# Head and end of a macaron encoder layer: first weights in halves, gains with x's first tile, products of ones, other places for the rows of x, root from a partial sum

## Chip, core and metric

The kernel runs on one core of a Trainium2 chip. The metric is the device time of one execution in microseconds (us). Before the change the median of 3 runs is 2106.32 us (2105.33 to 2113.24).

## What is computed

One layer of an encoder, on 256 tokens of width 2048, all in float32. Cut to what matters here:

```python
def layer(x, mem, ...):                                  # x: (1, 256, 2048)
    h = rms_norm(x, ffn1_norm)
    x = x + 0.5 * swiglu_ffn(h, ffn1_w_in, ffn1_w_out)   # w_in: 2048 x 11264, w_out: 5632 x 2048
    ...                                                  # two token mixers, then cross-attention to mem
    h = rms_norm(x, ffn2_norm)
    x = x + 0.5 * swiglu_ffn(h, ffn2_w_in, ffn2_w_out)
    return rms_norm(x, final_norm)

def rms_norm(x, g):
    return x * lax.rsqrt(jnp.mean(x * x, axis=-1, keepdims=True) + 1e-6) * g

def swiglu_ffn(h, w_in, w_out):
    gate, up = jnp.split(h @ w_in, 2, axis=-1)
    return (jax.nn.silu(gate) * up) @ w_out
```

## The kernel before

Every float32 product is made of three products of a faster format: each operand is split into a high part (a copy in that format) and a low part (operand minus high part). So each weight tile of 128 x 1024 goes through one CAST on ACT (ScalarE, the high part) and one subtraction on DVE (VectorE, the low part) before PE (TensorE) uses it. `split` and `parts` do this; `gained` does the same for one 128 x 256 tile of the transposed x, times the gain of the norm.

The first feed-forward, class `FeedForward`, is where the program starts. `run` goes over the 16 tiles of 128 features of x (k = 0 to 15, called tile 0 to tile 15 below) for the first group of 512 gate and 512 up columns (group 0). For each tile the function `x_arrives` loads x's part (two tiles per DMA) and calls `gained`, `raw` loads the weight tile (512 KB), `parts` splits it, and `by_two` makes 12 products of 512 columns. Then follow ten more groups (`group`, from `seven` and `eight`), in which some pairs of tiles take fewer products by combined operands; `sides` prepares these from x in the first group, and `summed` prepares a tile whose low part a DMA of the POOL queue forms by adding in memory.

The factor of the norm, one number per token, is applied behind the products (`give`). So the sums of squares of x are only needed at the end of group 0: `x_squares` loads four pieces of x by rows (512 KB each) and squares them on ACT, and `x_root` makes the root.

Weight tiles land in nine buffers in turn: four of the pool `wraw` (named raw) and five parts of the tile `spare`. `x_squares` takes its buffers from `wraw` too. The split tiles have five buffers: three named hl and two of the tile ring. All these loads are issued by the SP queue (SyncE). The engines run in order, and a scheduler sets the order of each engine's instructions when the program is built, from its own estimate of times.

The end is the last quarter of the second feed-forward's output and the final norm. The first three quarters of each token's sum of squares (`sums`, one column per quarter) are known some 60 us before the end. `give` adds the four columns, takes a Sqrt on ACT, improves it by one step on DVE, and scales and stores the rows, for the two halves of the tokens (t = 0, then t = 1).

Of the kernel before, what the change touches and what calls it, by code (L numbers as in the profile page):

```python
# [40 lines left out]

PV_SIZES = [
    ("ffn1_norm", KD), ("mix_norm", KD), ("xattn_norm", KD), ("mem_norm", KD), ("ffn2_norm", KD),
# [23 lines left out]
def layer(ctx: ExitStack, tc: tile.TileContext, a: dict):  # L67
# [118 lines left out]
    nc.vector.memset(ones, 1.0)  # L186
    nc.scalar.activation(out=st.tile([P, 1], F32, name="warm"), in_=ones[:, 0:1], func=AF.Silu)
    ident = const.tile([P, P], F32, name="ident")
    make_identity(nc, ident)
    pv = const.tile([P, NPV], F32, name="pv")  # L190
    xt = ctx.enter_context(tc.tile_pool(name="xt", bufs=1))
    xT = xt.tile([P, KD, T], F32, name="xT", tag="x")
# [44 lines left out]
    def gained(dst, k, x, g):  # L237

        nc.scalar.activation(out=dst[:, k, 0], in_=x, func=AF.Copy, scale=g)
        nc.vector.scalar_tensor_tensor(  # L240
            out=dst[:, k, 1], in0=x, scalar=g, in1=dst[:, k, 0].bitcast(F32), op0=ALU.mult, op1=ALU.subtract
        )

# [55 lines left out]
    class FeedForward:  # L299
# [62 lines left out]
        def sides(self, i):  # L362
# [4 lines left out]
            for q in range(2):  # L367
                nc.scalar.activation(out=xg[:, q], in_=xT[:, k + q], func=AF.Copy, scale=col(self.gain, k + q))
# [86 lines left out]
        def run(self, before, after, root, more=None):  # L455
# [3 lines left out]
            for k in range(KD):  # L459
                before(k)  # L460
                w = self.parts(self.raw(0, k))
# [57 lines left out]
    head = PV["mix_norm"][0]  # L519

    def x_squares(c):

        raw = wraw.tile([P, 1024], F32, name="raw")
# [3 lines left out]
    with ExitStack() as stack:  # L527
        ff = FeedForward(stack, ("S1", "S0", "S2"), x_hl, "ffn1_norm", a["ffn1_w_in"], PATTERNS[0], SUMMED[0])

        def x_arrives(k):  # L530
            if k % 2 == 0:
                nc.sync.dma_start(out=xT[:, k:k + 2], in_=a["xT"][:, k:k + 2])
            if k == 0:
                nc.sync.dma_start(out=pv[:, :head], in_=a["pv"][:, :head])
            gained(x_hl, k, xT[:, k], col("ffn1_norm", k))

        def x_more(k):
            if k == 6:
                nc.sync.dma_start(out=pv[:, head:], in_=a["pv"][:, head:])
            if k in (5, 7, 9, 11):  # L540
                x_squares(k // 2 - 2)
# [14 lines left out]
        turns = ff.run(x_arrives, x_more, x_root, x_given)  # L556
# [423 lines left out]
    with ExitStack() as stack:  # L980
        ff = FeedForward(stack, ("S0", "S1", "S2"), x_hl, "ffn2_norm", a["ffn2_w_in"], PATTERNS[1], SUMMED[1])
# [29 lines left out]
        eps = st.tile([P, 1], F32, name="eps")  # L1011
        nc.vector.memset(eps, RMS_EPS)

# [131 lines left out]
```

## Time and profile before

| | |
|---|---|
| Median of 3 runs | 2106.32 us (2105.33 to 2113.24) |
| The profiled execution | 2108.84 us |
| its span, first to last instruction | 2107.0 us |
| PE busy | 2084.5 us, 99% of the span |
| PE waits for another engine or a DMA | 12.6 us in all |
| first product of group 0 | at 7.11 us |
| first product of group 1 | at 57.53 us |
| last product of the program | starts at 2096.64 us |

The profiled execution is one run of its own, 2.5 us above the median; its span is 1.84 us shorter than its time. In the rows, L and a number is a line of the kernel before; a timeline row has the start, the duration, the engine, the line, output and inputs, how often it stands in a row, and in brackets how long the engine had been idle and what ended that. SPq and ACTq are the DMA-issuing parts of SP and ACT, so such a row is the issue and not the transfer. PEclk, the granted clock, is a share of full speed (1.00 is 2.4 GHz, 0.50 is 1.2 GHz).

### The profile page before, as it was taken

To read this page: it belongs to the slowest core of one execution; us is meant where nothing else is said; L and a number is where in the kernel's file an instruction comes from. 1 tells how busy PE (TensorE), PEld (TensorE's weight loads), DVE (VectorE), ACT (ScalarE), POOL (GpSimd) and SP (SyncE) were. 2 spreads that over 40 slices of the span, in tenths; PEclk is the share of its full clock that TensorE was granted. 3 is DMA by queue.
4 is the path that set the end of the run, shared out by engine and by line. 5 is a ranking of instruction groups with operands and counts; after the bars stand their busy time and mean duration, and the time that the engine had idled before them with its cause. 6 is when DMAs were issued, how large, how long until landed. Compare 5 with 4: busy or idle time off the path is not lost.

```text
span 2107.0 us, 26590 instructions
## 1 busy us (share of the span) xinstructions
PE 2084.5 (99%) x9764; PEld 1738.5 (83%) x9764; DVE 1576.8 (75%) x2215; ACT 1161.6 (55%) x1450; POOL 67.7 (3%) x83
## 2 busy tenths in 40 slices
PE   8999999999999999999999999999999999999998
PEld 6888888888888888888888888888888888888886
DVE  6888888876655589889877665777888887787754
ACT  7666566645544454445665454556665666554443
POOL 0000000000000000000000000000000000000000
PEclk9999999999999999999999999999999999999999
DMA  9778777855666676666565543686787778556664
GB/s 360 230 227 257 229 238 245 263 167 169 216 198 188 206 236 200 190 176 185 176 201 185 186 154 111 206 281 191 231 259 247 232 229 250 178 160 202 197 192 149
DMA packets 122244, 442.34 MB, mean 210 GB/s; under 512 B 13697, under 2 KB 13825, under 8 KB 121729
## 3 DMA queue, kind: packets, MB, share of 16 engines
q1 hardware_dynamic: 113184, 407.35, 58.8%
q0 software_dynamic: 8640, 32.51, 8.5%
q8 instruction: 76, 1.25, 0.2%
q10 hardware_dynamic: 288, 0.79, 0.1%
q14 instruction: 56, 0.45, 0.1%
HBM read 438.49 MB, written 2.10 MB: 209 GB/s over the span
## 4 chain that ended last, share of the span: by engine, by line
PE 84%; issue 11%; DMA 2%; ACT 1%; POOL 1%; DVE 1%; SPq 0%; POOLq 0%; ACTq 0%
PE acc L172 12%; PE acc L173 12%; PE acc L171 12%; PE acc L125 9%; PE acc L289 7%; PE acc L288 7%; PE acc L291 7%; PE acc L126 4%; PE acc L277 2%; PE acc L276 2%; PE acc L275 2%; PE aux L263 1%; PE acc L1066 1%; PE acc L1065 1%; PE acc L1067 1%
## 5 line engine op out<-in xcount | busy, mean ns | idle before, releaser
L113 DVE TENSOR_TENSOR hl<-raw,hl 128x1024 fp32r<-128x1024 f32 (+1 forms) x402 | 488.6, 1216 | 282.5 <-ACT hl L112 281.1
L112 ACT CAST hl<-raw 128x1024 fp32r<-128x1024 f32 (+1 forms) x402 | 419.7, 1045 | 481.6 <-PE acc L173 289.3
L339 ACT CAST hl<-spare 128x1024 fp32r<-128x1024 f32 (+1 forms) x135 | 131.8, 993 | 95.5 <-DVE spare L389 38.5
L340 DVE TENSOR_TENSOR hl<-spare,hl 128x1024 fp32r<-128x1024 f32 (+1 forms) x135 | 154.4, 1150 | 35.8 <-ACT hl L339 34.2
L288 PE MATMUL acc<-hl,x_hl 128*128 128x512 f32 x408 | 144.2, 394 | 9.7 <-ACT hl L339 9.7
L289 PE MATMUL acc<-hl,x_hl 128*128 128x512 f32 x408 | 149.9, 395 | 0.0
L340 DVE TENSOR_TENSOR hl<-raw,hl 128x1024 fp32r<-128x1024 f32 (+1 forms) x101 | 113.9, 1131 | 45.9 <-ACT hl L339 44.3
L339 ACT CAST ring<-spare 128x1024 fp32r<-128x1024 f32 (+1 forms) x99 | 97.2, 988 | 68.9 <-DVE spare L389 26.9
L340 DVE TENSOR_TENSOR ring<-spare,ring 128x1024 fp32r<-128x1024 f32 (+1 forms) x99 | 112.9, 1145 | 19.9 <-ACT ring L339 18.8
L291 PE MATMUL acc<-hl,x_hl 128*128 128x512 f32 x408 | 127.5, 392 | 0.0
L339 ACT CAST hl<-raw 128x1024 fp32r<-128x1024 f32 (+1 forms) x101 | 97.7, 977 | 51.8 <-PE acc L291 16.1
L172 PE MATMUL acc<-hl,x_hl 128*128 128x512 f32 x256 | 100.5, 392 | 0.2 <-DVE hl L113 0.2
L172 PE MATMUL acc<-hl,m_hl 128*128 128x512 f32 x256 | 100.4, 392 | 0.0
L173 PE MATMUL acc<-hl,m_hl 128*128 128x512 f32 x256 | 100.2, 391 | 0.0
L173 PE MATMUL acc<-hl,x_hl 128*128 128x512 f32 x256 | 99.8, 390 | 0.0
L288 PEld LDWEIGHTS acc<-hl,x_hl 128*128 128x128 f32 x408 | 76.8, 189 | 25.9 <-ACT hl L339 10.1
L289 PE MATMUL acc<-ring,x_hl 128*128 128x512 f32 x248 | 93.1, 389 | 0.0
L288 PE MATMUL acc<-ring,x_hl 128*128 128x512 f32 x248 | 91.2, 390 | 0.0
L171 PE MATMUL acc<-hl,m_hl 128*128 128x512 f32 x256 | 91.2, 393 | 0.0
L289 PEld LDWEIGHTS acc<-hl,x_hl 128*128 128x128 f32 x408 | 77.2, 190 | 16.9 <-DVE hl L340 1.1
L291 PEld LDWEIGHTS acc<-hl,x_hl 128*128 128x128 f32 x408 | 77.5, 190 | 16.4
L125 PE MATMUL acc<-x_hl,hl 128*128 128x512 f32 x256 | 91.0, 398 | 0.0
(359 smaller groups left out, 5173.9 us busy)
## 6 DMA issues: line engine op xcount, KB each, us to landing
spare<-in_ffn_w_in SPq DMA_DIRECT2D x192, 512.0 KB, 6.4
raw<-in_ffn_w_out SPq DMA_DIRECT2D x176, 512.0 KB, 3.8
raw<-in_ffn_w_in SPq DMA_DIRECT2D x160, 512.0 KB, 6.3
hl_s<-in_ffn_w_in POOLq DMA_DIRECT2D x44, 512.0 KB, 7.3
raw<-in_w_mix_vg SPq DMA_DIRECT2D x32, 512.0 KB, 4.6
raw<-in_w_k SPq DMA_DIRECT2D x32, 512.0 KB, 4.0
raw<-in_w_v SPq DMA_DIRECT2D x32, 512.0 KB, 4.4
raw<-in_w_mix_out SPq DMA_DIRECT2D x32, 512.0 KB, 4.6
```

The lines of the kernel that those rows point to most:

```text
L112: nc.scalar.copy(out=hl[:, 0, :size], in_=raw[:, :size])
L113: newest[0] = nc.vector.tensor_tensor(out=hl[:, 1, :size], in0=raw[:, :size], in1=hl[:, 0, :size].bitcast(F32), op=ALU.subtract)
L125: nc.tensor.matmul(acc, lhsT=w_hi, rhs=x_hl, start=first, stop=False, skip_group_check=True)
L126: nc.tensor.matmul(acc[:, 0], lhsT=w_lo, rhs=x_hl[:, 0], start=False, stop=last, skip_group_check=True)
L171: nc.tensor.matmul(acc[t], lhsT=x[:, 0, s], rhs=hi[:, k], start=k0 + k == 0, stop=False)
L172: nc.tensor.matmul(acc[t], lhsT=x[:, 0, s], rhs=lo[:, k], start=False, stop=False)
L173: nc.tensor.matmul(acc[t], lhsT=x[:, 1, s], rhs=hi[:, k], start=False, stop=k0 + k == nk - 1)
L288: nc.tensor.matmul(acc[t][g], lhsT=x[:, 0, s], rhs=hi[:, cols[g]], start=(t, g) in first, stop=False)
L289: nc.tensor.matmul(acc[t][g], lhsT=x[:, 0, s], rhs=lo[:, cols[g]], start=False, stop=False)
L291: nc.tensor.matmul(acc[t][g], lhsT=x[:, 1, s], rhs=hi[:, cols[g]], start=False, stop=last)
L339: nc.scalar.copy(out=hl[:, 0, :n], in_=raw[:, :n])
L340: newest[0] = nc.vector.tensor_tensor(out=hl[:, 1, :n], in0=raw[:, :n], in1=hl[:, 0, :n].bitcast(F32), op=ALU.subtract)
```

## The change

Head:

- The gains of the first norm leave the packed vector `pv` and come with x's first tile in one DMA (`gains_x0`, 128 x 272), issued by the ACT queue; x's second tile is a second DMA of that queue. The remainder of `pv` is one DMA instead of two.
- The first weight tile comes in two halves (`early`), each with its own DMA, CAST and subtraction, and the second half of the columns first. The splits are held behind the first `gained`.
- 11 products of a 128 x 128 tile of ones with itself (`WARM`) stand ahead of the first real product on PE. Nothing reads their result.
- The rows of x land in the tiles h 7 to h 4 in place of `wraw` buffers. These tiles hold results of groups 4 to 7 later. They are loaded beside tiles 2, 4, 6 and 8 and no longer beside tiles 5, 7, 9 and 11.
- `give` of group 0 stands ahead of the second `summed` in the program.

End: the first three columns of `sums` are added, scaled and raised by the epsilon early (`most`). Behind the last column follow a Sqrt with `most` as its bias, and two TENSOR_SCALAR with scalars from memory, in the place of a reduction, a TENSOR_SCALAR and a SCALAR_TENSOR_TENSOR.

```diff
...
+    gx = xt.tile([P, KD + KD * T], F32, name="gx", tag="x")
+    gains, xT = gx[:, :KD], gx[:, KD:].rearrange("p (k t) -> p k t", t=T)
+    nc.scalar.dma_start(out=gx[:, :KD + T], in_=a["gains_x0"])
+    nc.scalar.dma_start(out=xT[:, 1], in_=a["xT"][:, 1])
+    nc.vector.memset(ones, 1.0)
+    idle = pa.tile([P, 2, T], F32, name="aux")
+    for _ in range(WARM):
+        nc.tensor.matmul(idle[:, 0, :P], lhsT=ones, rhs=ones, start=True, stop=True)
...
+        def early(self, before):
+
+            self.raw_at += 1
+            self.at += 1
+            raw = wraw.tile([P, 1024], F32, name="raw")
+            hl = whl.tile([P, 2, 1024], F32R, name="hl")
+            halves = [slice(G, 2 * G), slice(0, G)]
+            for s in halves:
+                nc.sync.dma_start(out=raw[:, s], in_=self.w_in[0, :, 0, s])
+            x = before(0)
+            for s in halves:
+                with tc.issue_after(x.ins):
+                    split(hl[:, 0, s], hl[:, 1, s], raw[:, s])
+            return hl
...
+            self.give(0, [acc[t][0] for t in range(2)], [acc[t][1] for t in range(2)], r)
             if more is not None:
                 more()
                 self.summed(1)
-            self.give(0, [acc[t][0] for t in range(2)], [acc[t][1] for t in range(2)], r)
...
     def x_squares(c):
-        raw = wraw.tile([P, 1024], F32, name="raw")
+        raw = ff.h[7 - c].rearrange("p a b -> p (a b)")
...
         def x_arrives(k):
-            if k % 2 == 0:
+            if k > 0 and k % 2 == 0:
                 nc.sync.dma_start(out=xT[:, k:k + 2], in_=a["xT"][:, k:k + 2])
-            if k == 0:
-                nc.sync.dma_start(out=pv[:, :head], in_=a["pv"][:, :head])
...
-            if k in (5, 7, 9, 11):
-                x_squares(k // 2 - 2)
+            if k in (2, 4, 6, 8):
+                x_squares(k // 2 - 1)
...
-            nc.vector.reduce_sum(out=tot, in_=sums[:, t], axis=AX.X)
-            nc.scalar.activation(out=s, in_=tot, func=AF.Sqrt, scale=1.0 / D, bias=eps)
-            nc.vector.tensor_scalar(out=v, in0=tot, scalar1=1.0 / D, scalar2=RMS_EPS, op0=ALU.mult, op1=ALU.add)
+            last = sums[:, t, 3:4]
+            nc.scalar.activation(out=s, in_=last, func=AF.Sqrt, scale=1.0 / D, bias=most[t])
+            nc.vector.tensor_scalar(out=v, in0=last, scalar1=1.0 / D, scalar2=most[t], op0=ALU.mult, op1=ALU.add)
             nc.vector.reciprocal(out=r, in_=s)
-            nc.vector.scalar_tensor_tensor(out=r, in0=v, scalar=r, in1=s, op0=ALU.mult, op1=ALU.add)
+            nc.vector.tensor_scalar(out=r, in0=v, scalar1=r, scalar2=s, op0=ALU.mult, op1=ALU.add)
...
+        most = [st.tile([P, 1], F32, name=f"f_most{t}") for t in range(2)]
+        for t in range(2):
+            nc.vector.reduce_sum(out=most[t], in_=sums[:, t, 0:3], axis=AX.X)
+            nc.vector.tensor_scalar(
+                out=most[t], in0=most[t], scalar1=1.0 / D, scalar2=RMS_EPS, op0=ALU.mult, op1=ALU.add
+            )
```

What the built programs show at the places of which the prediction speaks, lines as in the kernel that is meant. On the SP queue, the first loads before (raw and spare are weight tiles, `in_x` the rows of x):

```order
L532 DMA xT<-in_xT 128x512
L534 DMA pv<-in_pv 128x16
L349 DMA raw<-in_ffn_w_in 128x1024 x2
L532 DMA xT<-in_xT 128x512
L349 DMA raw<-in_ffn_w_in 128x1024 x2
L532 DMA xT<-in_xT 128x512
L349 DMA spare<-in_ffn_w_in 128x1024 x2
L532 DMA xT<-in_xT 128x512
L349 DMA spare<-in_ffn_w_in 128x1024
L539 DMA pv<-in_pv 128x352
L524 DMA raw<-in_x 128x1024
```

and now (gx is x's transposed tile with the gains):

```order
L477 DMA raw<-in_ffn_w_in 128x512 x2
L363 DMA raw<-in_ffn_w_in 128x1024
L563 DMA gx<-in_xT 128x512
L363 DMA raw<-in_ffn_w_in 128x1024
L555 DMA h_127<-in_x 128x1024
L363 DMA raw<-in_ffn_w_in 128x1024
L563 DMA gx<-in_xT 128x512
L363 DMA spare<-in_ffn_w_in 128x1024
L555 DMA h_126<-in_x 128x1024
L363 DMA spare<-in_ffn_w_in 128x1024
```

The first rows of x moved from behind tile 6 to ahead of tile 3, the second (which stood behind tile 8, below this piece) to ahead of tile 5.

On ACT, in the later half of group 0, before (L525 is the last square of x's rows, L204 the Sqrt of `x_root`):

```order
L339 CAST hl<-raw 128x1024
L358 ACTIVATE more<-spare 128x1024
L359 CAST more<-spare 128x1024
L525 ACTIVATE raw,x_tot<-raw 128x1024
L339 CAST hl<-raw 128x1024
L339 CAST hl<-spare 128x1024
L204 ACT_TABLE_LOAD
L204 ACTIVATE rt_426<-rv_425 128x2
```

and the same instructions now (L556 the last square, L217 the Sqrt, L252 `gained`):

```order
L556 ACTIVATE h_124,x_tot<-h_124 128x1024
L353 CAST ring<-raw 128x1024
L123 CAST ring<-spare 128x4x128
L217 ACT_TABLE_LOAD
L217 ACTIVATE rt_437<-rv_436 128x2
L252 ACTIVATE x_hl<-gx 128x256 x2
L353 CAST hl<-raw 128x1024 x2
```

The last square stood ahead of the CAST of tile 12 and stands ahead of that of tile 9; the Sqrt with its table load stood behind the CAST of tile 15 (hl<-spare) and stands ahead of those of tiles 10 and 11.

## Rows read from the trace of the kernel before

**Rows 1.** the page: busy time, share of the span and instructions of each engine

```profile
PE 2084.5 (99%) x9764; PEld 1738.5 (83%) x9764; DVE 1576.8 (75%) x2215; ACT 1161.6 (55%) x1450; POOL 67.7 (3%) x83
```

**Rows 2.** PE waits of the whole program: us in total, times, longest us

```profile
PE acc L288 <- ACT hl L339: 9.7, 2, 7.1
PE acc L275 <- ACT h L418: 0.5, 1, 0.5
```

**Rows 3.** busy time by stretch (with instructions), granted clock, DMA share, GB/s

```profile
0.00:7.11 7.11, 0.00 (x1) 0.00 (x1) 2.16 (x9) 4.69 (x10) 0.70 (x6) 1.00 0.72 220
7.11:17.17 10.06, 10.06 (x36) 8.16 (x36) 9.46 (x15) 8.75 (x14) 0.00 (x0) 1.00 1.02 385
17.17:30.00 12.83, 12.83 (x58) 10.65 (x57) 11.31 (x21) 12.26 (x23) 0.00 (x0) 1.00 1.03 405
```

**Rows 4.** timeline of the head: start us, us, what, count [idle before <-releaser]

```profile
1.65 0.90 SPq L349 DMA_DIRECT2D raw<-in_ffn_w_in  x2
3.83 0.91 ACT L239 ACTIVATE x_hl<-xT,pv 128x256 fp32r<-128x256 f32 x2 [1.13 <-DMA pv<-in_pv]
4.65 0.89 ACT L368 ACTIVATE spare<-xT,pv 128x256 f32<-128x256 f32 x2
6.01 1.04 ACT L339 CAST hl<-raw 128x1024 fp32r<-128x1024 f32 x1 [0.47 <-DMA raw<-in_ffn_w_in]
6.96 0.61 ACT L120 CAST ring<-spare 128x512 fp32r<-128x512 f32 x1
7.11 2.07 PE L288 MATMUL acc<-hl,x_hl 128*128 128x512 f32 x4 [7.11 <-ACT hl L339]
11.55 1.05 ACT L339 CAST ring<-raw 128x1024 fp32r<-128x1024 f32 x1 [0.24 <-DMA raw<-in_ffn_w_in]
11.96 1.07 PE L288 MATMUL acc<-hl,x_hl 128*128 128x512 f32 x4
17.39 0.39 PE L288 MATMUL acc<-ring,x_hl 128*128 128x512 f32 x1
31.00 0.39 PE L288 MATMUL acc<-ring,x_hl 128*128 128x512 f32 x1
```

**Rows 5.** DMA issue at 30.12 us: count, KB, us to landing

```profile
raw<-in_x SPq DMA_DIRECT2D x1, 512.0 KB, 12.5
```

**Rows 6.** the stall of tile 12, from the timeline

```profile
41.63 0.61 PE L291 MATMUL acc<-hl,x_hl 128*128 128x512 f32 x2
42.69 1.06 ACT L525 ACTIVATE raw<-raw 128x1024 f32<-128x1024 f32 x1 [1.92 <-DMA raw<-in_x]
43.65 0.19 ACT L525 ACTIVATION_READ_ACCUMULATOR raw<-raw 128x1 f32 x1
44.82 1.50 PE L288 MATMUL acc<-hl,x_hl 128*128 128x512 f32 x4 [2.58 <-ACT hl L339]
```

**Rows 7.** granted clock behind the stall: us, PE busy, clock, DMA share, GB/s

```profile
46.00:47.00 1.00, 1.00 (x3) 0.50 1.04 266
```

**Rows 8.** from group 0 to group 1, from the timeline

```profile
45.73 1.28 ACT L204 ACT_TABLE_LOAD   x1
47.03 0.20 ACT L204 ACTIVATE rt<-rv 128x2 f32<-128x2 f32 x1
57.53 0.39 PE L275 MATMUL acc<-ring 128*128 128x512 f32 x1
```

**Rows 9.** products of 128 columns in f32, by form: busy us, mean ns

```profile
L774 PE MATMUL aux<-wT,vs 128*128 128x128 f32 x32 | 4.4, 274 | 0.0
```

**Rows 10.** chain behind the last product, from the timeline

```profile
2099.40 0.16 DVE L1025 TENSOR_REDUCE f_tot<-sums 128x1 f32<-128x4 f32 x1 [0.79 <-ACT sq L1019]
2099.59 0.29 ACT L1026 ACTIVATE f_s<-f_tot,eps 128x1 f32<-128x1 f32 x1 [0.22 <-DVE f_tot L1025]
2100.11 0.60 DVE L1029 SCALAR_TENSOR_TENSOR f_r<-f_v,f_r,f_s 128x1 f32<-128x1 f32 x1
```

**Rows 11.** one-column TENSOR_SCALAR with a scalar from memory, by form

```profile
L898 DVE TENSOR_SCALAR mx<-mx,r_t 128x1 f32<-128x1 f32 x8 | 1.7, 207 | 0.1
```

More of the change, by code (lines that the diff above doesn't have):

```diff
@@ L39 @@
 SUMMED = ((2, 7, 13), (2, 7, 13))
+WARM = 11
 PV_SIZES = [
-    ("ffn1_norm", KD), ("mix_norm", KD), ("xattn_norm", KD), ("mem_norm", KD), ("ffn2_norm", KD),
+    ("mix_norm", KD), ("xattn_norm", KD), ("mem_norm", KD), ("ffn2_norm", KD),
     ("conv_b", NCT), ("conv_ln_g", NCT), ("conv_ln_b", NCT), ("out_norm_conv", NCT),
@@ L185, in layer @@
     ones = const.tile([P, P], F32, name="ones")
-    nc.vector.memset(ones, 1.0)
-    nc.scalar.activation(out=st.tile([P, 1], F32, name="warm"), in_=ones[:, 0:1], func=AF.Silu)
     ident = const.tile([P, P], F32, name="ident")
-    make_identity(nc, ident)
     pv = const.tile([P, NPV], F32, name="pv")
     xt = ctx.enter_context(tc.tile_pool(name="xt", bufs=1))
-    xT = xt.tile([P, KD, T], F32, name="xT", tag="x")
+    gx = xt.tile([P, KD + KD * T], F32, name="gx", tag="x")
[6 more added lines that the diff above has]
+        nc.tensor.matmul(idle[:, 0, :P], lhsT=ones, rhs=ones, start=True, stop=True)
+    nc.scalar.activation(out=st.tile([P, 1], F32, name="warm"), in_=ones[:, 0:1], func=AF.Silu)
+    make_identity(nc, ident)
     def col(name, k):
@@ L237, in gained @@
     def gained(dst, k, x, g):
-        nc.scalar.activation(out=dst[:, k, 0], in_=x, func=AF.Copy, scale=g)
+        part = nc.scalar.activation(out=dst[:, k, 0], in_=x, func=AF.Copy, scale=g)
         nc.vector.scalar_tensor_tensor(
@@ L242, in gained @@
         )
+        return part
     def gained_tile(tag):
@@ L367, in sides @@
             for q in range(2):
-                nc.scalar.activation(out=xg[:, q], in_=xT[:, k + q], func=AF.Copy, scale=col(self.gain, k + q))
+                nc.scalar.activation(out=xg[:, q], in_=xT[:, k + q], func=AF.Copy, scale=self.gain(k + q))
             a11, a21, a12, a22 = xg[:, 0, :P], xg[:, 0, P:], xg[:, 1, :P], xg[:, 1, P:]
@@ L453, in group, with run @@
             self.give(j, (p1, u2), (u4, u5), r)
-        def run(self, before, after, root, more=None):
+        def early(self, before):
[11 more added lines that the diff above has]
+            return hl
+        def run(self, before, after, root, more=None, early=False):
             acc = token_accs()
@@ L459, in run @@
             for k in range(KD):
-                before(k)
-                w = self.parts(self.raw(0, k))
+                if k == 0 and early:
+                    w = self.early(before)
+                else:
+                    before(k)
+                    w = self.parts(self.raw(0, k))
                 begin = [(t, g) for t in range(2) for g in range(2)] if k == 0 else []
@@ L554, in x_given @@
             ff.hls.append(more[:, 2:])
-        turns = ff.run(x_arrives, x_more, x_root, x_given)
+        turns = ff.run(x_arrives, x_more, x_root, x_given, early=True)
         xT = xt.tile([P, KD, T], F32, name="xT", tag="x")
```

14 lines of the change are left out of this document (6 added, 8 removed).

## The prediction

> **What bounds the kernel now.** I read the busy table first: PE is busy for 99% of the span [rows 1], and its waits are 12.6 us in all. The list of PE's waits says where: 9.7 us in two waits for the CAST of a first-group tile, 7.1 of them at the start [rows 2]. So between group 0 and the end of the program there is next to nothing to win, and what the head gives is kept, since PE carries every later stage: the gain is the shift of the first product of group 1, plus what the end gives.
>
> The stretches show why the head is slow: the DMA engines are full from 7 to 30 us, at 385 and 405 GB/s [rows 3]. At 405 GB/s a 512 KB tile takes 1.29 us. PE uses one weight tile in 2.72 us: from tile 3 at 17.39 to tile 8 at 31.00 it is 13.61 us for five [rows 4]. So transfers run ahead of PE later, but not for the first tiles. Tile 0 cost PE 4.85 us, 7.11 to 11.96 [rows 4], where 2.72 would do: its products ran at the half level. Then the timeline has one more hole: the last product of tile 11 starts near 41.86, and tile 12 starts at 44.82 after 2.58 us of idle PE [rows 6]. ACT stood at the square of the fourth rows of x, whose DMA took 12.5 us from issue to landing [rows 5], and the CAST of tile 12 was queued behind it. After that idle time the granted clock shows 0.50, the 1.2 GHz level [rows 7]. From tile 3 to the first product of group 1 it is 57.53 - 17.39 = 40.14 us [rows 4, 8], where 13 tiles need 35.36: 4.8 us lost, 2.6 idle and 2.2 by the clock.
>
> **Part by part.**
>
> *Start.* Before, tile 0 waits for a chain: x's tile and the gains, both ahead of the weights on SP, release `gained` at 3.83, and the weights, issued from 1.65 on, release the CAST at 6.01 [rows 4]. Now 401 KB (gains, tile 0 of x, half the weights) replace 776 KB ahead of the first product. In the first 7.11 us 220 GB/s flowed [rows 3], 1.56 MB. The first half should land near 4.0 us, its CAST take about 0.6 (the same size as L120 [rows 4]), so that PE starts at about 4.7. This alone is worth little, for the next tiles are bound by bytes. Tile 1's bytes are complete as before (7.4 us), tile 2's too (about 10.2). Tile 3 now has 512 KB of rows of x ahead: its CAST before waited for its landing until 11.55 [rows 4]; 1.29 more is about 12.9, and with a CAST of 1.05 its first product comes at 14.0 at the earliest; I add 0.5 for the low part, which DVE begins when the CAST ends, and take 14.5. Gain 17.39 - 14.5 = 2.9. If PE is still at the half level through tile 0 and part of tile 1, tile 3 starts at about 15.7, gain 1.7; the upper bound is 14.0, gain 3.4.
>
> *Products of ones.* 32 such products took 4.4 us at the full level, 0.14 each [rows 9]; at the half level 11 are about 3 us, from 1.0 (when the ones are written) to 4. They end before the first real product, so they cost nothing, and if they raise the clock early, they save up to 12 x 0.2 us on tile 0. Of this tile 3's bytes let through 1.2 at most, the difference above. The Trainium skill (TensorE: Matmul & The Clock Gate, What's actually happening) says that the default is the half level and that activity releases it; the rows agree, since tile 0 ran slow from PE's first work on. By this sentence any products count, and 14.5 holds; if products of ones did not count, it would be 15.7 and the sum 1.2 us less.
>
> *Rows of x in h.* They no longer hold two `wraw` turns of weight tiles, and the fourth is behind tile 8 on SP and no longer behind tile 12's load. So the 12.5 us landing no longer stands ahead of tile 12's CAST: the 4.8 us go. What is late next: the squares now stand ahead of the CASTs of tiles 3, 5, 7 and 9, and the Sqrt with its table load ahead of tile 10's. From 12.9 on ACT has until tile 10: 8 CASTs of 1.05, 4 `gained` pairs of 0.91, 2 pairs for `sides` of 0.89 [rows 4], 3 squares of 1.06 and 0.19 [rows 6], 2 CASTs of 0.61 and the load with the root, 1.48 [rows 8]: 20.2 us, so 33.1. Tile 10 is needed at 14.5 + 7 x 2.72 = 33.5. It fits with 0.4 to spare. The row shows the root's ACTIVATE at 47.03, 0.02 behind the load's end [rows 8]. The Trainium skill (ScalarE: Activation LUTs, What ACT_TABLE_LOAD costs) gives 1.38 us of DRAIN on top of a load; by it tile 10 would come 1 us late and the sum be 1 us less. The trace disagrees, and the measurement decides.
>
> *Group 0 to group 1.* PE would now end group 0 at 14.5 + 35.4 = 49.9, 7.6 us earlier. The second tile of group 1 has to be there some 3.2 us before (three CASTs): 46.7. Up to it SP moves 14.9 MB; 1.56 MB are moved by 7.11, the rest at about 400 GB/s takes to 40.4; the accumulating DMA of `summed` adds 512 to 1024 KB, 1.3 to 2.6 us, and a landing can lag behind the flow by 2 to 5 us while it runs (the 12.5 us of [rows 5] against eight tiles of 1.29). So it lands between 44 and 49. I take 0.8 us of new wait, bounds 0 and 3. The wait for the first Silu of `give`, 0.5 [rows 2], starts behind a table load that stands where it stood: no change, at most 0.8 gained by the new place of `give`.
>
> *End.* The reduction and its handover go: 2099.40 to 2099.59, 0.19. The SCALAR_TENSOR_TENSOR of 0.60 [rows 10] becomes a TENSOR_SCALAR; with one scalar from memory such a one took 0.207 [rows 11], two are perhaps 0.27. So 0.5 us in all, between 0.2 (if the two scalars cost as the old form) and 0.6. The early sums of `most` stand on DVE in a stretch where it waits for PE: nothing.
>
> **Sum.** 2.9 + 4.8 - 0.8 + 0.5 = 7.4 us. Against the profiled execution that is 2108.84 - 7.4 = 2101.4. That execution lay 2.5 us above the median of the runs, so the median should fall from 2106.32 to about 2099.0. A measurement of this kernel tells about 0.5%, 10.5 us, from no change; so this counts as within 0.5%.
>
> **Rivals.**
>
> 1. *The handover to group 1 is starved.* Being earlier, PE meets the landing of group 1's first tiles while the accumulating DMA runs. For: the bound of 49 us above; DMA is full until then. Against: the four rows of x no longer hold raw buffers, so the loads are issued sooner. Price 3 us of wait, and 2.2 more if the clock falls as after the 2.58 us hole. It leaves a gain of 3.0 to 5.2: 2101 to 2103.3. Chance 0.18.
>
> 2. *The squares stall ACT as the fourth one did* (slower). Place: the four squares ahead of the CASTs of tiles 3, 5, 7 and 9. Each that waits for its rows as L525 did costs 4.8 us (2.6 idle, 2.2 clock). Without them the gain is 2.9 + 4.8 + 0.5 = 8.2; from the second on the kernel is slower, with two by 1.4 (2107.7), with four by 11 (2117.3). For: rows of x now go ahead of weights while DMA is full. Against: on SP each stands directly ahead of the tile whose CAST follows it, so ACT waits little longer than it would for that tile. One stall 0.05 (2103), two or more 0.04.
>
> 3. *It does what it says and more.* Tile 3 at 14.0, no wait at the handover, the Silu's wait gone: 3.4 + 4.8 + 0.5 + 0.8 = 9.5: 2096.8; over 10.5 only if the first tiles also land faster than bytes say. Chance 0.10, of it 0.05 beyond 0.5%.
>
> **How the numbers follow.** The forecast itself (2097 to 2101) has 0.63. The range reaches from rival 3 without its last part to rival 1 and a single stall: 2095.0 to 2104.0; the second rival's slower cases and a surprise on the fast side are left out. Faster by over 0.5%: 0.07 (rival 3, and 0.02 for bytes that I overrate). Slower by over 0.5%: 0.03, three or more stalls. Within: 0.90.
>
> **What would show it.** In the changed profile the first real product should stand near 4.7, tile 3 near 14.5, and no PE wait for a CAST near tile 12. The first product of group 1 should stand near 50.7, against 57.53. The end from the last quarter's square to the last store should be 0.5 shorter. Wrong would be: tile 3 after 16 us, a PE wait of more than 1 us between tiles 3 and 15, a granted clock of 0.50 after 15 us, or group 1 later than 53 us.

## The result, and the profile after

The changed kernel takes 2111.82 us (median of 16 runs, 2110.66 to 2113.52), against 2106.47 for the kernel before in the same series (16 runs, 2104.55 to 2113.24). The ratio is 1.0024, with a 95% interval of 1.0016 to 1.0031: 5.3 us slower, where 7.4 us faster were forecast. That is within the 0.5% that the prediction counts as no change, but the interval leaves out 1, and the time lies 7.8 us above the upper end of the range.

PE is as busy as before, and only for longer. The page of the changed kernel answers [rows 1]: busy time, share of the span and instructions of each engine.

```profile
PE 2098.4 (99%) x9786; PEld 1741.5 (83%) x9786; DVE 1576.9 (75%) x2217; ACT 1162.5 (55%) x1451; POOL 67.7 (3%) x83
```

PE's busy time rose from 2084.5 to 2098.4 us, 13.9 us, and the 22 added MATMULs (the products of ones) are 4.6 of them. PE's waits after the change are 3.3 us in all, against 12.6 before. Three of the six rows (us in total, times, longest), which answer [rows 2]:

```profile
PE aux L203 <- DVE ones L200: 1.1, 1, 1.1
PE acc L289 <- ACT h L432: 0.5, 1, 0.5
PE acc L303 <- DVE hl L124: 0.2, 1, 0.2
```

The 9.7 us of waits for a CAST are gone. The head came out close to the forecast; its timeline answers [rows 4] and [rows 8] (start us, duration us, what, count, idle before):

```profile
1.06 4.55 PE L203 MATMUL aux<-ones 128*128 128x128 f32 x22 [1.06 <-DVE ones L200]
4.79 0.60 ACT L123 CAST hl<-raw 128x512 fp32r<-128x512 f32 x1
5.44 0.50 PE L302 MATMUL acc<-hl,x_hl 128*128 128x512 f32 x1
11.77 1.05 ACT L353 CAST ring<-raw 128x1024 fp32r<-128x1024 f32 x1 [0.16 <-DMA raw<-in_ffn_w_in]
14.25 1.07 PE L302 MATMUL acc<-ring,x_hl 128*128 128x512 f32 x4
49.61 0.39 PE L289 MATMUL acc<-ring 128*128 128x512 f32 x1
```

Tile 3 starts at 14.25 (forecast 14.5), and the first product of group 1 at 49.61, 7.9 us before the 57.53 of [rows 8]. From there to the end of the span it was 2107.0 - 57.53 = 2049.5 us before, and it is 2110.5 - 49.61 = 2060.9 after: 11.4 us are lost behind group 0, where nothing had been forecast to change. The end itself is not the place; it became 1.1 us shorter (worked out with the last run below), so the products in between lose some 12.5. The rows of the end answer [rows 10]:

```profile
2103.55 0.21 DVE L1053 TENSOR_SCALAR f_v<-sums,f_most 128x1 f32<-128x1 f32 x1 [0.79 <-ACT sq L1045]
2104.07 0.27 DVE L1055 TENSOR_SCALAR f_r<-f_v,f_r,f_s 128x1 f32<-128x1 f32 x1
2104.58 1.35 DVE L1065 TENSOR_SCALAR spare<-spare,f_r 128x512 f32<-128x512 f32 x3
```

Where the 11.4 us went is seen when the products are listed by the tiles they read. Each row is a line of code and a pair of operands: count, duration in ns as minimum/median/maximum, first and last start in us. First the kernel before:

```profile
L288 PE MATMUL acc<-more,x_hl x96: 388/389/390, 76.5 to 440.9; 128*128 128x512 f32 x96
L288 PE MATMUL acc<-hl_s,x_hl x176: 387/389/402, 59.9 to 1825.5; 128*128 128x512 f32 x176
L171 PE MATMUL acc<-hl,hC x112: 389/389/398, 532.0 to 2036.3; 128*128 128x512 f32 x112
```

Then the changed kernel, the same three groups:

```profile
L302 PE MATMUL acc<-more,x_hl x96: 392/396/398, 68.8 to 438.3; 128*128 128x512 f32 x96
L302 PE MATMUL acc<-hl_s,x_hl x176: 391/397/400, 52.0 to 1828.3; 128*128 128x512 f32 x176
L174 PE MATMUL acc<-hl,hC x112: 390/396/398, 529.6 to 2040.6; 128*128 128x512 f32 x112
```

In each of these the median is 7 to 8 ns longer, and even the shortest is longer than the median was. `hl_s` holds the tiles of `summed` and later the first tiles of h, `more` takes the place of x's tile after group 0, and `hC` holds the last tiles of h. There are 1494 products that pair one of these with another tile: 720 of hl_s, 402 of more, 372 of hC. From start to start they take 233.4 ns in the mean, against 226.9 before: some 9.6 us, most of the loss. The products that read none of them (hl or ring with x_hl, hA or hB, for instance) keep their median of 227 ns, but not quite their mean: in some 5900 of them it goes from 227.1 to 227.6, another 3 us. It is back at 227.1 in the run below that restores the places; how it comes about, no run shows.

None of these lines was edited. What they share is their place in memory. `more`, `hl_s` and `hC` (and `held`, which is multiplied with `hC` alone and so kept its distance) are allocated behind the pool of small tiles `st`; hl, ring, x_hl, hA and hB lie ahead of it. The change moved both sides: `pv` lost 16 columns (64 bytes), `st` lost a net 32 bytes (eps and f_tot out, f_most in), and x's slot got the gains (64 bytes more). So `hl_s` and `hC` moved by 32 bytes against the tiles ahead of `st`, and `more` by as much the other way.

The rows also say who is involved. These are rows of the changed kernel from the last products of `hC` (rows of PE and PEld between them left out):

```profile
2096.03 0.63 PE L1099 MATMUL acc<-hl,hC 128*128 128x512 f32 x2
2098.80 0.69 DVE L1041 SCALAR_TENSOR_TENSOR spare<-acc,spare 128x512 f32<-128x512 f32 x1 [5.82 <-PE acc L1101]
2098.83 0.40 PE L1099 MATMUL acc<-hl,hC 128*128 128x512 f32 x1
2099.52 0.63 ACT L1045 ACTIVATE sq<-spare 128x512 f32<-128x512 f32 x1 [7.80 <-DVE spare L1041]
```

Up to 2098.8 DVE had been idle for 5.82 us and ACT for over 7, and no DMA packet moved from 2092 to 2100. Still the 12 starts from 2096.03 to 2098.83 take 2.80 us, 0.233 each, as slow as in the middle of the program. The same 12 in the kernel before take 2.72 us, 0.227 each (the first and the last of them):

```profile
2091.43 0.62 PE L1065 MATMUL acc<-hl,hC 128*128 128x512 f32 x2
2094.15 0.39 PE L1065 MATMUL acc<-hl,hC 128*128 128x512 f32 x1
```

So no other engine and no transfer makes these products slow: it is PE alone, with its two operands.

### The profile page after: what moved, and what is told of

Its sections match the earlier page's. It is cut to its first block, busy times and chain, and to the rows that moved or that the text cites. A ratio compares the mean times of both kernels' runs of the same rounds, so it can differ in the third digit from the quotient of the medians.

```text
span 2110.5 us, 26638 instructions
## 1 busy us (share of the span) xinstructions
PE 2098.4 (99%) x9786; PEld 1741.5 (83%) x9786; DVE 1576.9 (75%) x2217; ACT 1162.5 (55%) x1451; POOL 67.7 (3%) x83
## 3 DMA queue, kind: packets, MB, share of 16 engines
q10 hardware_dynamic: 576, 1.06, 0.1%
## 4 chain that ended last, share of the span: by engine, by line
PE 90%; issue 7%; DMA 1%; ACT 1%; POOL 1%; DVE 1%; DVEq 0%; POOLq 0%; ACTq 0%
PE acc L176 12%; PE acc L175 12%; PE acc L174 12%; PE acc L128 9%; PE acc L303 8%; PE acc L302 8%; PE acc L305 8%; PE acc L129 4%; PE acc L290 3%; PE acc L289 3%; PE acc L291 3%; PE aux L277 1%; PE aux L290 1%; PE aux L291 1%; PE aux L289 1%
## 5 line engine op out<-in xcount | busy, mean ns | idle before, releaser
L303 PE MATMUL acc<-hl,x_hl 128*128 128x512 f32 x408 | 147.5, 391 | 0.2 <-DVE hl L124 0.2
L302 PE MATMUL acc<-hl,x_hl 128*128 128x512 f32 x408 | 141.9, 391 | 0.0
L305 PE MATMUL acc<-hl,x_hl 128*128 128x512 f32 x408 | 127.1, 390 | 0.0
L175 PE MATMUL acc<-hl,x_hl 128*128 128x512 f32 x256 | 100.5, 393 | 0.3 <-DVE hl L116 0.3
L176 PE MATMUL acc<-hl,x_hl 128*128 128x512 f32 x256 | 100.0, 390 | 0.0
L303 PE MATMUL acc<-ring,x_hl 128*128 128x512 f32 x248 | 91.7, 390 | 0.0
L128 PE MATMUL acc<-y_hl,hl 128*128 128x512 f32 x256 | 90.5, 399 | 0.0
L128 PE MATMUL acc<-o_hl,hl 128*128 128x512 f32 x256 | 90.4, 399 | 0.0
L303 PEld LDWEIGHTS acc<-hl,x_hl 128*128 128x128 f32 x408 | 76.2, 188 | 16.9 <-DVE hl L124 0.5
L174 PE MATMUL acc<-hl,x_hl 128*128 128x512 f32 x256 | 90.0, 392 | 0.0
```

The lines of the kernel that those rows point to most:

```text
L128: nc.tensor.matmul(acc, lhsT=w_hi, rhs=x_hl, start=first, stop=False, skip_group_check=True)
L174: nc.tensor.matmul(acc[t], lhsT=x[:, 0, s], rhs=hi[:, k], start=k0 + k == 0, stop=False)
L175: nc.tensor.matmul(acc[t], lhsT=x[:, 0, s], rhs=lo[:, k], start=False, stop=False)
L176: nc.tensor.matmul(acc[t], lhsT=x[:, 1, s], rhs=hi[:, k], start=False, stop=k0 + k == nk - 1)
L302: nc.tensor.matmul(acc[t][g], lhsT=x[:, 0, s], rhs=hi[:, cols[g]], start=(t, g) in first, stop=False)
L303: nc.tensor.matmul(acc[t][g], lhsT=x[:, 0, s], rhs=lo[:, cols[g]], start=False, stop=False)
```

## Experiments

The first pair asks whether the place is the cause, with an edit that adds no instruction. Theory A: operands off a multiple of 64 bytes are slower. Rival B: the work that the change adds makes the products slower. In the changed kernel:

```diff
-    st.tile([P, 8], F32, name="to_64")
+    st.tile([P, 16], F32, name="to_64")
```

> The changed kernel with one edit: the padding tile at the head of the pool of small tiles is 16 columns instead of 8, 32 bytes more, so that every tile allocated behind that pool (x's tile and the fourth slot that takes its place, hl_s, hC, held) starts on a multiple of 64 bytes again, as before the change. Not one instruction is added or moved. Theory A (a product whose operand starts 32 bytes past a multiple of 64 is slower): the 1506 products that read hl_s, more, hC or held go back from 234 ns a start to 227, which takes 1506 x 7.1 ns = 10.7 us off 2111.8, and up to 2 us more for the products between them: 2099.0 to 2101.1, faster than the kernel before by 5 to 8 us, and the first product of group 1 still starts at 49.6. Rival B (the products are slower for what the change adds or moves: the products of ones, the accumulators shifted by one buffer, other work beside them): nothing moves, 2111.8, products of hl_s at 234 ns.

Measured: 2108.0 us (ratio to before 1.0003, 0.9994 to 1.0012), 3.8 us faster than the changed kernel, but not back. The groups, of `more`, `hl_s` and `hC`:

```profile
L302 PE MATMUL acc<-more,x_hl x96: 389/389/398, 69.1 to 435.1; 128*128 128x512 f32 x96
L302 PE MATMUL acc<-hl_s,x_hl x176: 388/394/398, 52.4 to 1825.7; 128*128 128x512 f32 x176
L175 PE MATMUL acc<-hl,hC x112: 393/398/401, 526.6 to 2038.5; 128*128 128x512 f32 x112
```

`more` is fast again, `hl_s` only in part, and `hC` is about as slow as it was, though all three start on a multiple of 64. Theory A falls as it stands: with this edit `hl_s` and `hC` start at the very address of the kernel before. What differs from before is where the other operand is, 64 bytes lower.

The same edit in the kernel before:

> The kernel before with the same edit and nothing else: there it moves the same tiles off the multiple of 64 by 32 bytes. Theory A: the 1506 products go from 227 to 234 ns a start, 10.7 to 13 us slower, 2117 to 2119.5; the head stays as it was, the first product of group 1 at 57.5. Rival B: no change, 2106.5.

Measured: 2120.72 us, ratio 1.0060 (1.0046 to 1.0074), 13.5 us slower (1.2 us above the range expected), with no instruction added or moved. The group of `more`, as an example, stands at 395:

```profile
L288 PE MATMUL acc<-more,x_hl x96: 391/395/401, 74.0 to 443.8; 128*128 128x512 f32 x96
```

So rival B falls too: a shift of 32 bytes alone costs the kernel before more than the change did. Two runs then moved the three tiles by distances of their own, in the kernel before:

```diff
-            self.hls = [self.own.tile([P, 2, 1024], F32R, name="hl_s")]
+            own = self.own.tile([P, 2 * 1024 + 16], F32R, name="hl_s")
+            self.hls = [own[:, 4:4 + 2048].rearrange("p (two n) -> p two n", two=2)]
...
-            more = xt.tile([P, 4, 1024], F32R, name="more", tag="x")
+            more = xt.tile([P, 4 * 1024 + 16], F32R, name="more", tag="x")
+            more = more[:, 8:8 + 4096].rearrange("p (four n) -> p four n", four=4)
...
-                    self.hC = pool.tile([P, KF - 36, 2, T], F32R, name="hC")
+                    hC = pool.tile([P, (KF - 36) * 2 * T + 16], F32R, name="hC")
+                    self.hC = hC[:, 8:8 + (KF - 36) * 2 * T].rearrange("p (k two t) -> p k two t", two=2, t=T)
```

> The kernel before with three tiles shifted one by one inside a slot that is 64 bytes larger, so that nothing else leaves its multiple of 64: `more` (only ever the moving operand) by 32 bytes, hC (only ever the stationary operand) by 32 bytes, hl_s (moving in the first product of a block, stationary for four rows of the second) by 16 bytes. Theory A in its wide form (either operand counts, and any offset from a multiple of 64): products of more, hC and hl_s all at 234 ns a start (duration 396 instead of 389 in the groups). In its narrow form (only what the array streams, the moving operand, counts): more 234, hC 227. If a multiple of 16 bytes is enough at 16 but not at 32, hl_s stays at 227; that has no reason in the rows, and is the outcome that would speak against a boundary at all. Rival C (what counts is how far hl_s, hC and more lie from the tiles before the pool, not a boundary; here the distance of each differs): no common pattern. Time by the wide form: 2106.5 + 10.7 = 2117; by the narrow 2106.5 + (402 + 528) x 7.1 ns = 2113.

> As the run with three tiles shifted one by one, with other sizes: `more` by 4 bytes, hC by 16 bytes, hl_s by 48 bytes. Theory A, wide form: a product reads 64 bytes at a time, and any start off a multiple of 64 costs one more read, so all three at 234 ns a start whatever the size of the offset. If the cost goes by the size of the offset, 4 bytes cost less than 48. If only the middle, 32, costs, all three stay at 227.

Measured: 2117.75 and 2116.78 us, one run each. These expectations think in multiples of 64 and overlook that the larger slots move the tiles behind them by another 64 and 128 bytes. Against the operands ahead of `st`, the first run moved `more` by 32, `hl_s` by 80 and `hC` by 160, all slow, with `hC`, only ever the loaded operand, as slow as `more`, only ever the streamed one. (In the trace a LDWEIGHTS loads 128 columns of the one operand, and a MATMUL streams 512 columns of the other past it.) The second moved them by 4, 112 and 144 (in a pair of operands, the streamed one is named first):

```profile
L288 PE MATMUL acc<-more,x_hl x96: 393/398/403, 74.1 to 444.3; 128*128 128x512 f32 x96
L288 PE MATMUL acc<-hl_s,x_hl x176: 387/391/404, 57.3 to 1832.0; 128*128 128x512 f32 x176
L171 PE MATMUL acc<-hl,hl_s x56: 392/395/482, 478.6 to 1989.3; 128*128 128x512 f32 x56
L171 PE MATMUL acc<-hl,hC x112: 388/390/401, 535.5 to 2043.8; 128*128 128x512 f32 x112
```

Here `hC` starts 16 bytes off a multiple of 64 and is fast, and `more`, 4 bytes off, is the slowest of all. Neither the multiple of 64 nor the size of the offset orders these rows.

That leaves theory A2: what counts is the distance of the streamed from the loaded operand, modulo some power of two. The kernel before has all of them at distance 0 modulo 512. Four runs test it. The first brings the changed kernel back to distance 0:

```diff
-    st.tile([P, 8], F32, name="to_64")
...
-            more = xt.tile([P, 4, 1024], F32R, name="more", tag="x")
+            more = xt.tile([P, KD + 4 * 1024], F32R, name="more", tag="x")
+            more = more[:, KD:].rearrange("p (four n) -> p four n", four=4)
```

> The changed kernel with the operands of its products brought back into step and nothing else: the padding tile (32 bytes) is left out and `more` lies 64 bytes into its slot, so that the start of every tile that a product reads (x_hl, hl, ring, more, hl_s, hC, held) is the same modulo 512 bytes, as in the kernel before. Theory A2 (a product is slower when the operand it streams and the operand that is loaded beside it start at different places modulo some 2^n bytes; the multiple of 64 itself does not matter): all products back at 227 ns a start, so the head's 7.9 us and the end's 0.5 stay: 2106.5 - 8.4 = 2098.1, range 2097 to 2100. Theory A (only the multiple of 64 counts): as in the run with 64-byte starts, 2108.0. Rival B (a part of the loss is the work that the change adds): between, 2100 to 2108, with products of hl_s or hC still above 227 ns.

Measured: 2101.71 us (2098.8 to 2103.25), ratio to before 0.9972 (0.9961 to 0.9982). Against the changed kernel, by the two ratios, that is 0.9972 / 1.0024 = 0.9948, some 11 us faster, and 5.3 us faster than the kernel before. The range that was expected with A2, 2097 to 2100, is missed by 1.7 us (the section on the prediction says where the head's gain was taken too large), but no group of `hl_s`, `hC` or `more` is left above 227 ns from start to start, as rival B would have had it. All three are back:

```profile
L301 PE MATMUL acc<-more,x_hl x96: 389/389/389, 69.2 to 433.7; 128*128 128x512 f32 x96
L301 PE MATMUL acc<-hl_s,x_hl x176: 387/389/402, 52.6 to 1820.8; 128*128 128x512 f32 x176
L173 PE MATMUL acc<-hl,hC x112: 387/389/397, 524.7 to 2032.0; 128*128 128x512 f32 x112
```

The second moves every tile of the kernel before by 32 bytes, and no distance:

```diff
+    const.tile([P, 8], F32, name="by_32")
     ones = const.tile([P, P], F32, name="ones")
```

> The kernel before with a padding tile of 32 bytes at the very front, so that every tile starts 32 bytes later, on no multiple of 64, while no distance between two operands changes. Theory A2 (the distance between the operands counts): nothing changes, 2106.5, 227 ns a start. Theory A (the multiple of 64 counts): all 7500 long products at 234 ns, over 50 us slower.

Measured: 2107.24 us, ratio 1.0002 (0.9993 to 1.0011), no change, every operand 32 bytes off a multiple of 64:

```profile
L289 PE MATMUL acc<-more,x_hl x96: 389/389/390, 73.5 to 438.0; 128*128 128x512 f32 x96
```

The third and fourth ask for the period, with larger steps of the same edit (`more`, `hl_s`, `hC` moved by 64, 128, 256, then by 128, 256, 384):

> The kernel before with three tiles moved against the rest by different distances: `more` by 64 bytes, hl_s by 128, hC by 256. It asks by which distance the slowing repeats. Theory A2 with a period of 64: all at 227 ns; of 128: more at 232 to 234, the others 227; of 256: only hC at 227; of 512 or more: none.

> As the run in steps of 64, with `more` moved by 128 bytes, hl_s by 256, hC by 384. Theory A2 with a period of 64 or 128: all at 227 ns; of 256: only hl_s at 227; of 512: none. If the same distance costs more in one tile than in another, it is not the distance alone that counts.

Measured: 2115.42 and 2109.53 us, one run each. First the run in steps of 64, then that in steps of 128:

```profile
L288 PE MATMUL acc<-more,x_hl x96: 388/394/398, 73.9 to 442.8; 128*128 128x512 f32 x96
L288 PE MATMUL acc<-hl_s,x_hl x176: 387/395/399, 57.1 to 1831.4; 128*128 128x512 f32 x176
L171 PE MATMUL acc<-hl,hC x112: 388/389/398, 534.1 to 2042.6; 128*128 128x512 f32 x112
```

```profile
L288 PE MATMUL acc<-more,x_hl x96: 387/398/404, 73.8 to 441.1; 128*128 128x512 f32 x96
L288 PE MATMUL acc<-hl_s,x_hl x176: 388/389/395, 57.1 to 1825.1; 128*128 128x512 f32 x176
L173 PE MATMUL acc<-hl,hC x112: 389/395/477, 532.8 to 2037.2; 128*128 128x512 f32 x112
```

The fast group is `hC` in one and `hl_s` in the other, each time the one moved by 256. So the cost repeats with 256 bytes and goes with the distance, not with the tile. All runs together, by the distance modulo 256, taken as the start of the streamed operand minus that of the loaded one. A tile that was moved by 32 bytes thus counts at 32 where it is streamed and at 224 where it is loaded. The last column is the median duration; a group has three lines, and their span is given:

| distance, bytes | where | median, ns |
|---|---|---|
| 0 | all three tiles before, in step and with all moved by 32; `more` of the 64-byte run; `hC` and `hl_s` when moved by 256 | 389 |
| 4 | `more`, streamed | 398 to 399 |
| 32 | `hl_s` of the change, `more` and `hl_s` moved by 32, streamed | 395 to 397 |
| 64 | `hl_s` of the 64-byte run and `more`, streamed | 392 to 394 |
| 80 | `hl_s`, streamed | 392 |
| 96 | `hC`, loaded | 393 to 399 |
| 112 | `hl_s`, streamed; `hC`, loaded | 390 to 393 |
| 128 | `hl_s` and `more`, streamed; `hC` and `hl_s`, loaded | 392 to 398 |
| 144 | `hl_s`, loaded | 394 to 395 |
| 176 | `hl_s`, loaded | 393 to 396 |
| 192 | `hC` and `hl_s` of the 64-byte run, loaded | 393 to 398 |
| 224 | `more` of the change, streamed; `hC` and `hl_s` of the change, loaded | 396 |

Only 0 is at 389. The distance 112 is the cheapest of the others, with `hC` (moved by 144) as with `hl_s` streamed (moved by 112), while the same `hl_s` loaded, at 144, costs 394 to 395 in the same run: so it is the difference of the two starts that orders the rows, and not how far a tile was moved. Why 112 costs least, no run shows. The table holds for these groups. There are 768 other products of 512 columns, which stream `x_hl`, `y_hl` or `o_hl` past a loaded `hl` and take turns with products of 256 columns; they are at distance 0 in every run and still have medians of 391 to 399, in the kernel before 395 to 398.

The last four runs measure the parts of the change, with operands in step, so that nothing else moves. First the products of ones (`WARM = 0`):

> The kernel with its operands in step, without the 11 products of ones. Theory of the prediction (they bring the clock to its full level before the first real product, at no cost): the first real product stays at 5.4 us, since it waits for the cut of the first weights (CAST, to 5.39 in the changed kernel); the granted clock rises some 4 us after it, as in the kernel before (4.3 us, 7.11 to 11.4), so 4.1 us at 0.43 us a start instead of 0.227 cost 4.1 x (1 - 0.227/0.43) = 1.9 us: first product of group 1 at 51.5 to 52, time 2101.7 + 1.9 = 2103.6. Rival: the products of ones delay the first real product or its waits, and without them it starts earlier: then the loss is under 1 us, 2102 to 2102.7.

Measured: 2100.28 us, ratio to before 0.9969 (0.9957 to 0.9980); with them it was 0.9972 (0.9961 to 0.9982). The first real product starts with the end of the CAST, and without the ones PE goes at 0.43 us a start, not 0.227, up to 11.03 (rows between are left out):

```profile
5.47 0.80 PE L301 MATMUL acc<-hl,x_hl 128*128 128x512 f32 x1 [5.47 <-ACT hl L122]
10.21 0.63 PE L302 MATMUL acc<-hl,x_hl 128*128 128x512 f32 x1
10.63 0.56 PE L304 MATMUL acc<-hl,x_hl 128*128 128x512 f32 x1
11.03 1.08 PE L301 MATMUL acc<-hl,x_hl 128*128 128x512 f32 x4
51.86 0.39 PE L288 MATMUL acc<-ring 128*128 128x512 f32 x1
```

The granted clock reads 1.00 in this stretch, as it does for the kernel before in [rows 3]. That the slow pace is the half level is read from the pace: 0.43 us a start is also what PE shows behind the stall of tile 12, where the granted clock reads 0.50 [rows 7]. The kernel in step, with the ones, has these rows:

```profile
1.06 5.06 PE L202 MATMUL aux<-ones 128*128 128x128 f32 x22 [1.06 <-DVE ones L199]
4.64 0.60 ACT L122 CAST hl<-raw 128x512 fp32r<-128x512 f32 x1
5.77 0.77 PE L301 MATMUL acc<-hl,x_hl 128*128 128x512 f32 x1
7.85 1.05 ACT L352 CAST hl<-raw 128x1024 fp32r<-128x1024 f32 x1 [0.78 <-DMA raw<-in_ffn_w_in]
```

Here the CAST is through at 5.24, but the ones hold PE until 5.77: they delay the first real product by some 0.5 us, as the rival has it. The delay does not last, since tile 1 waits for its bytes until 7.85. In the changed kernel there is no delay (the CAST ends at 5.39, the product starts at 5.44).

Group 1 begins at 51.86, against 50.24 with the ones: 1.6 us, where 1.9 were expected. The time does not show it: in these two profiled executions the program from there on took 2098.8 - 51.86 = 2046.9 us and 2101.5 - 50.24 = 2051.3. Of these 4.4 us, 0.5 is the wait for the Silu at the handover, which is gone without the ones; 1.1 are shorter waits for tiles of `hl_s` (0.6 against 1.7) and 0.3 a shorter one for `p_hl`. Another 1.0 lies in the stage that reads `o_hl`: the median of its products of 512 columns is 395 ns without the ones and 398 with them, though code, operands and distances are the same. The levels stand there elsewhere too: 395 in the kernel before and with the old end, 398 in the changed kernel, 391 with the first tile as a whole. That they are no effect of the ones is an inference; why the level changes stays open. The two ratios to before differ by less than their intervals, so whether the 1.6 us of the head, or the 1.1 that are left of them behind the handover, are kept to the end is not shown.

Then the rows of x back in `wraw`, beside tiles 5, 7, 9 and 11:

```diff
-        raw = ff.h[7 - c].rearrange("p a b -> p (a b)")
+        raw = wraw.tile([P, 1024], F32, name="raw")
...
-            if k in (2, 4, 6, 8):
-                x_squares(k // 2 - 1)
+            if k in (5, 7, 9, 11):
+                x_squares(k // 2 - 2)
```

> The kernel with its operands in step, with the rows of x once more in the four buffers of raw weights and squared behind tiles 5, 7, 9 and 11, as in the kernel before. Theory of the prediction (a row load holds a buffer of raw weights, and tile 12 waits for it, 2.6 us of idle time and 2.2 us at the half level): PE waits 2 to 3 us between tiles 8 and 13, the clock falls to 0.50 once, first product of group 1 at 49.6 + 4.8 = 54.4, time 2101.7 + 4.8 = 2106.5. Rival (the stall came from the late start of the first tile, and an earlier start takes it away by itself): no wait over 0.5 us, 2101.7.

Measured: 2102.67 us (0.9981, 0.9971 to 0.9990), group 1 at 51.95, 1.7 us later than with the rows in h. PE waits at tiles 11 and 12, but for short times, and the granted clock reads 1.00 throughout. It waits once more at the handover:

```profile
36.47 1.20 PE L301 MATMUL acc<-hl,x_hl 128*128 128x512 f32 x4 [0.23 <-ACT hl L352]
40.36 1.21 PE L301 MATMUL acc<-hl,x_hl 128*128 128x512 f32 x4 [0.30 <-ACT hl L352]
54.89 0.50 PE L288 MATMUL acc<-hl,x_hl 128*128 128x512 f32 x1 [1.27 <-ACT h L431]
```

The last of these waits is for the Silu and is 0.5 in step. It is longer here because ACT stood 7.13 us for the bytes of a tile of group 1, so that the CASTs ahead of the Silu came late. Together that is 2.5 us of loss, so both accounts miss: there is a loss, but not of 4.8. Of the times, 0.9981 and 0.9972 of the kernel before, the intervals overlap. How the old head stalls in other executions is seen in the six kernels with the head of before that ran here. Their group 1 begins at 54.65, 54.74, 54.77, 54.77, 55.00 and 55.06, not at 57.53. The row of tile 12, in the kernel with all tiles moved by 32:

```profile
43.28 1.20 PE L289 MATMUL acc<-hl,x_hl 128*128 128x512 f32 x4 [1.29 <-ACT hl L340]
```

Its idle time is 1.29 us, against 2.58 in [rows 6], and the granted clock stays at 1.00: from tile 11 at 38.90 to tile 13 at 46.48 it takes 7.58 us instead of 5.44, a loss of 2.1. In the other five the same stretch loses 1.2 to 1.9.

The first tile of weights as a whole (`run` without `early`):

> The kernel with its operands in step, with the first tile of weights loaded and cut as a whole, as in the kernel before; norm scales and x's first tile still come first on the second queue, and the products of ones are there. Theory of the prediction (halves bring the first product forward by the wait for the other half and by half a cut): first real product at 6.3 to 7.1 instead of 5.4, tile 3 some 1.0 to 1.7 us later, time 2102.7 to 2103.4; if the clock falls back in the idle time between the ones and the first product, up to 2 us more. Rival (the start is bound by the loads' landing, which halves do not change): under 0.5 us.

Measured: 2100.49 us in one run. The first real product starts at 6.43, against 5.77 with halves in step and 5.44 in the changed kernel; tile 3 at 14.98 against 14.88 and 14.25, group 1 at 50.34 against 50.24 and 49.61. So halves are worth 0.1 to 0.7 us, near the rival. What takes the rest differs: in step, tile 1 waits for its bytes (above); with the whole tile PE starts later and then goes from tile 1 on at its own pace (tile 3 starts 2.72 us behind tile 2). One thing more changes with `early`: the splits are no longer held behind the first `gained`, and the first product here waits for x's tile, which ACT does behind the CAST.

The end of the kernel before, on the new head:

> The kernel with its operands in step, with the end of the kernel before (the sum of all four parts after the last one, root with an eps tile, the second factor from memory). Its small tiles take 32 bytes more, and x's slot is made 224 bytes larger, so that all operands are in step here too. Theory of the prediction: the chain behind the last product is 0.5 us longer (0.2 to 0.6) than with the new end, the rest the same: 2102.2, a difference that the rows of the end show and the time does not. Rival (the root is not on the path, or the new end's wait for the last part costs as much as it saves): 0.

Measured: 2101.38 us in one run. The rows of its end:

```profile
2092.15 0.16 DVE L1054 TENSOR_REDUCE f_tot<-sums 128x1 f32<-128x4 f32 x1 [0.79 <-ACT sq L1048]
2093.71 1.28 DVE L1068 TENSOR_SCALAR spare<-spare,f_r 128x512 f32<-128x512 f32 x3
```

From the first of these to the second it is 1.56 us; in the changed kernel 1.03, so 0.53 per half of the tokens. The halves follow each other on DVE, and the second cannot be added up before the first's chain is through: the two add-ups lie 3.28 us apart after the change (2098.80 and 2102.08) and 3.81 before (2094.12 and 2097.93). So the saving counts twice, 1.06 us. From the start of the last product to the end of the span it is 10.22 us here and 9.22 in step, which agrees.

## Why the prediction failed

The sum of 7.4 us was 2.9 + 4.8 - 0.8 + 0.5, from an assumption made ahead of it: "what the head gives is kept, since PE carries every later stage". **That is the step that failed.** PE did carry every later stage, but its own products became slower. The change shrinks `pv` and `st` and lengthens x's slot, and each of these moves operands against one another. The prediction counted instructions, waits and bytes, and gave an allocation no cost. Its price was 11.4 us in the profiled execution, and 11 by the ratios with and without it. Without it the changed kernel stands at 2101.71, 2.7 above the forecast and inside its range.

The terms, one by one:

- **Start, 2.9.** Right in size, but in part by luck: tile 3 at 14.25 against a forecast of 14.5, gain 3.1. The forecast let tile 3 wait for its bytes until 12.9 and for its CAST until 14.0. Its CAST ran from 11.77 to 12.82, and PE came to it 1.4 us later. From 6.17 on PE waits for nothing in group 0: tile 3 comes at 14.25 because the first real product came at 5.44 and not at 4.7 (`gained` waited for x's tile until 4.37), and tile 0 took 3.33 us and not 2.72. Two errors, bytes too slow and a start too early, cancel. (Of the two loads compared there, the 401 KB are 392 in the unit of the 776.) In step, bytes do bind, at tile 1. That the pace of tile 0 matters was right: without the ones group 1 comes 1.6 us later, where the forecast had 1.2.
- **Products of ones, 3 us from 1.0 to 4.** Mis-sized: the 32 of [rows 9] are MATMULs, two for each of 16 products, so 0.14 us was half a product. 11 products became 22 MATMULs, 0.21 us each while slow, 4.55 us in all in the changed kernel and 5.06 in step, and end at 5.6 and 6.1. They cost nothing in the changed kernel, and 0.5 us of the first real product in step, which the wait for tile 1 hides. The Trainium skill (TensorE: Matmul & The Clock Gate, What's actually happening) says that activity releases the half level; the pair of runs agrees for products whose result nobody reads, by the pace: 0.227 us a start from tile 0's later products on with them, and 0.43 without.
- **Stall of tile 12, 4.8.** Right in mechanism, mis-sized. It was read from one execution in which the stall was long enough for the clock to fall; in six others with the same head it cost 1.2 to 2.1 us. The gain at the first product of group 1 is 7.9 against that one execution and 5.0 to 5.5 against the six. The excess was counted twice: the prediction takes all 4.8 us from a profile that lies 2.5 us above the median, and then takes the 2.5 us off once more to come to the median. That the stall is most of this excess is seen beside the kernel with all tiles moved by 32: of the 3.3 us between the two spans, 2.9 lie ahead of group 1.
- **Handover to group 1, -0.8.** Did not come: the changed kernel waits 0.5 there, for the Silu as before. Rival 1 did not happen in it (with the rows of x in `wraw` a wait of 1.3 us did), nor did rival 2 (no PE wait over 0.2 us within group 0).
- **End, 0.5.** Right per half of the tokens, but it counts for both: 1.06.

With these sizes, 4.4 to 5.5 from the head (group 1 starts at 50.24 in step and at 49.61 in the changed kernel) and 1.1 from the end, the kernel in step should gain some 5.5 to 6.6; measured are 5.3, with 3.8 to 8.2 in the interval. The range was missed because no rival held a slower product: the two slower ones were mechanisms of waits, and the list of what would show the forecast wrong named the starts of tile 3 and group 1, waits and clock levels. None of its four marks came, and the kernel is slower all the same.

## What to carry to other kernels

When a change touches the size of any tile or pool, compare the starts of the matmul operands before and after, modulo 256 bytes, also those of tiles that the change never names; here one spare tile of 32 bytes decided 13 us. A stage that PE bounds is not safe because its instructions are unchanged: look at the median duration of products by operand pair, not only at waits. And a stall that is read from a single execution should be priced with and without its clock drop; where that execution lies above the median, part of the stall is that excess and must not be counted again.

## What the runs showed of the hardware

In the groups of the table a product of 512 columns takes 389 ns when its streamed and its loaded operand start at the same place modulo 256 bytes, and 390 to 399 at the eleven other distances that were tried. The absolute place does not matter (all tiles moved by 32 bytes: ratio 1.0002), and either operand may be the one that is moved. It happens while DVE, ACT and the DMAs are idle (12 starts in 2.80 us, against 2.72 before). The Trainium skill (TensorE: Matmul & The Clock Gate, Step-by-step: what each phase is for) says that PE has a read port for each of the two and that loading the next weights takes nothing from the running product. That sentence has no place for a cost that depends on where the two operands start; the runs show one of some 7 ns a product, and the measurement decides. That the two reads meet in the memory is the likely reading, but no run here shows the mechanism. The products of the attention stage fit: both their operands (k_hl and q_hl, for one) lie behind `st`, were moved together, and keep their median of 283 ns.
